# Own score buffers, a later second and third search, and output weights rounded on GpSimd, in a two-layer decoder trunk

## The chip, the cores and the metric

One core of a Trainium2 chip runs the whole forward pass. The metric is the time of one execution on the device in microseconds (us). Three runs of the kernel before are shown, and one more execution was recorded by the hardware profiler. TensorE multiplies matrices, VectorE and ScalarE do elementwise work and reductions, GpSimd does small elementwise work and issues loads on a queue of its own, SyncE (SP) issues the other transfers.

## The reference

Two layers, each a mixer and a SwiGLU, with a layer norm around each. The change touches the first mixer alone, sparse attention over 1024 positions: eight indexer heads score every causal key, each query keeps its 256 best, and 16 heads in two key groups attend to those.

```python
h = x @ w_in
c_q, k, v, k_idx, w_idx = jnp.split(h, ...)
c_q = rms_norm(c_q, g_cq)
q, q_idx = c_q @ w_uq, c_q @ w_iq
...                                        # layer norm of k_idx, rope
def attend_block(args):                    # 128 queries
    rel = relu(einsum('bqhd,bsd->bhqs', qib, k_idx))
    score = where(causal, einsum('bqh,bhqs->bqs', wb, rel), -inf)
    _, sel = lax.top_k(score, 256)
    valid = sel <= t_pos
    ...                                    # k_sel, v_sel: the chosen keys
    logits = einsum('bqgrd,bqkgd->bqgrk', qg, k_sel) * 64 ** -0.5
    p = softmax(where(valid, logits, -inf))
    return einsum('bqgrk,bqkgd->bqgrd', p, v_sel)
out = lax.map(attend_block, ...)
return out @ w_o
```

## The kernel before

The 1024 positions are eight tiles of 128 queries. The gather of the reference is replaced by a mask: for each tile an array `bias` (queries by causal keys) holds 0 for a chosen key and a huge value for another, and attention runs over all causal keys. Tiles 0 and 1 have at most 256 causal keys and need no choice. Tiles 2 to 7 need three steps.

**Index.** `index(j)` computes the scores of tile j: for each of eight indexer heads and each chunk of keys (one chunk up to tile 3, two from tile 4 on), three matmuls (high and low parts of the operands), a Relu on ScalarE (L1406), and an accumulation on VectorE into the score buffer `sc` (L1409 for the first head, L1411 for the others). Operands `it` are loaded from device memory on GpSimd's queue (L1392), two loads for two heads. A chunk is one step of the generator: 8, 8, 16, 16, 16, 16 steps for tiles 2 to 7.

**Search.** `search((3, 2))`, `((5, 4))` and `((7, 6))` find the 256th best score of each query, two tiles at a time, one on ScalarE and one on VectorE. Ten rounds of bisection count the scores above a bound (L1479, L1480). The finish (L1493 to L1501) copies the scores below the bound into a scratch tile (`za`, `zv`), takes the best eight of them (MAX8), replaces them (MATCH_REPLACE8), and writes the mask with a Relu on ScalarE. A verdict follows: a column `bad` is sent through a small transfer (L1512) to one row, GpSimd sums it (L1517), and only if it isn't zero a repair, `search_all`, runs inside a branch (L1520). Whatever reuses a buffer of the search waits for that branch, whether it is entered or not. A search is 25 steps.

**Attention.** `att_main` runs tiles 0 to 7, for each the two key groups (half tiles), for each eight heads: logits on TensorE (L1775), mask and minimum on VectorE (L1777), Exp on ScalarE (L1779), transposes (L1746), copies (L1748), the product with V (L1751). At the end of a half tile VectorE inverts the sums (L1785). From tile 6 on V is used in split form: `values()` casts its eight key tiles into score and scratch buffers that are free by then (L1689 on ScalarE, the low part L1690 on VectorE). The query operands `qt` are loaded on GpSimd's queue (L1676), four heads ahead. The output weights W_o are loaded in the second half of tile 0 (L1590, SP's queue), and `prepare` (L1596, L1597) splits them into high and low parts in the first half of tile 1: the high part a rounding on ScalarE, the low part a subtraction on VectorE, and then SP loads x into the same place (L1599). `att_out` (matmuls into `W`, L104 to L106) multiplies a finished tile with them.

**What sets the order.** Before attention comes `att_in`, the projections, by a list written out by hand (`ORDER_IN`); at each `a` in it, `STEPS` says how many steps of the index and the search generators follow. In attention, after each head, `PLAN[j]` gives the index and search steps per head of tile j, added up until a whole step is due. At the end of a tile the next tile's search is driven to its end if it isn't done. That is the order in which the program is written. The tile framework then orders each engine's instructions ahead of time: what was written earlier goes first, but work that it takes to be ready is pulled forward where it takes an engine to be idle. The score buffers are `sc0` to `sc3`, tile j in `sc{j % 4}`: tile 6 takes over tile 2's and tile 7 tile 3's, and `indexes` holds tiles 6 and 7 back until the search of tiles 2 and 3 is written and five further slots have passed (`s.now`, `s.ended`).

Of the kernel before, what the change touches and what calls it, by code (L numbers as in the profile page):

```python
# [10 lines left out]
F32 = mybir.dt.float32  # L11
F32R = mybir.dt.float32r
BF16 = mybir.dt.bfloat16
F16 = mybir.dt.float16
# [7 lines left out]
P = 128  # L22
# [39 lines left out]
class Core:  # L62
# [1104 lines left out]
        q4 s1 a k3 q5 s4 a a s5 a q6 a a q7 s6 a a s7 a a"""  # L1167
    STEPS = [(4, 0), (4, 0), (4, 0), (4, 1), (0, 2), (4, 2), (4, 2), (4, 2), (5, 2), (4, 3), (5, 3), (5, 3), (5, 3), (5, 0)]

    PLAN = [(1, 0.4), (0.6, 0.4), (0.8, 0.5), (0.4, 0.5), (0, 1), (0, 1), (0, 0), (0, 0)]  # L1170
    LATE = [10, 3, 3, 6, 8, 5, 11]

    def att_in(self, ap, csp, tp, x):
# [186 lines left out]
            s.stored = max(s.stored, t)  # L1360

        s.idx_ps = self.ps_c
        s.index, s.find, s.stored, s.now = self.indexes(), self.searches(), -1, 0
        steps = iter(self.STEPS)

        def advance():
            s.now += 2
            for gen, n in zip((s.index, s.find), next(steps)):
                for _ in range(n):
                    next(gen, None)  # L1370
# [10 lines left out]
    def index(self, j):  # L1381

        nc, v, gp, s = self.nc, self.nc.vector, self.nc.gpsimd, self.att
        bp = s.sel
        nch, n = self.chunks(j)
        S = nch * n
        sc = self.tile(bp, [P, S], F32, f"sc{j % 4}")

        def load(k):
            it = [self.tile(bp, [P, 2, P], F32R, f"it{i}", bufs=2) for i in range(2)]  # L1390
            for i in range(2):
                gp.dma_start(it[i], s.ids[j][i][:, 2 * k : 2 * k + 2, :])  # L1392
            return it

        its = [load(0)]
        for h in range(8):
            if h % 2 == 0 and h < 6:
                its.append(load(h // 2 + 1))
            w = s.wi[:, j, h : h + 1]
            for c in range(nch):  # L1400
                kr = slice(c * n, (c + 1) * n)
                ps = s.idx_ps()[:, :n]
                it = tuple(x[:, h % 2, :] for x in its[h // 2])
                self.mm3(ps, it, (s.kih[:, kr], s.kil[:, kr]), True, True)
                r = self.tile(bp, [P, n], F32, "rel", bufs=2)
                nc.scalar.activation(r, ps, AF.Relu)  # L1406
                o = sc[:, kr]
                if h == 0:
                    v.tensor_scalar(o, r, w, 0.0, op0=ALU.mult, op1=ALU.add)  # L1409
                else:  # L1410
                    v.scalar_tensor_tensor(o, r, w, o, op0=ALU.mult, op1=ALU.add)  # L1411
                if h == 7 and c == nch - 1:
                    last = sc[:, S - P :]
                    gp.affine_select(last, last, [[-1, P]], ALU.is_ge, LOWEST, base=0, channel_multiplier=1)
                    s.sc[j] = sc
                yield

    def indexes(self):
        for j in range(2, NT):
            s = self.att  # L1420
            while j > s.stored or (j >= 6 and (j - 4 not in s.done or s.now < s.ended + 5)):
                yield
            yield from self.index(j)

# [28 lines left out]
    def search(self, js):  # L1453


        nc, v, gp, s = self.nc, self.nc.vector, self.nc.gpsimd, self.att
        bp = s.sel
        scs = [s.sc.pop(j) for j in js]
        Sa, Sv = (sc.shape[1] for sc in scs)
        small = lambda tag, *shape, dt=F32, **kw: self.tile(bp, [P, *(shape or (2,))], dt, tag, **kw)  # L1460
        z = [self.tile(bp, [P, T], F32, x) for x in ("za", "zv")]
        st, mv, sd = small("sst", 2, 2, 6), small("smv", 2, 2), small("ssd")
        for i, (j, sc) in enumerate(zip(js, scs)):
            m = 1 if j * P <= 512 else 2
            n = j * P // m
            for c in range(m):
                v.bn_stats(st[:, i, c, :], sc[:, c * n : (c + 1) * n])
            v.bn_aggr(mv[:, i, :], st[:, i, :m, :].rearrange("p a b -> p (a b)"))
            yield
        v.tensor_scalar(sd.bitcast(I32), mv[:, :, 1].bitcast(I32), 0.5, 532676608.0, op0=ALU.mult, op1=ALU.add)  # L1470
        wide, half = small("wide", 1), small("half", self.ROUNDS)
        v.tensor_tensor(wide, sd[:, 0:1], sd[:, 1:2], op=ALU.max)
        v.tensor_scalar(half, s.halves[:, : self.ROUNDS], wide, None, op0=ALU.mult)
        cnt, rej, at = (small(x, bufs=2) for x in ("cnt", "rej", "at"))
        v.scalar_tensor_tensor(at, s.starts[:, js[1] : js[1] + 2], wide, mv[:, :, 0], op0=ALU.mult, op1=ALU.add)
        yield
        junk = [s.bias[j] for j in js]
        for k in range(self.ROUNDS):
            nc.scalar.activation(junk[0], scs[0], AF.Sign, bias=at[:, 0:1], scale=-1.0, accum_out=cnt[:, 0:1])  # L1479
            v.tensor_scalar(  # L1480
                junk[1], scs[1], at[:, 1:2], float(Sa - Sv - TOPK), op0=ALU.is_lt, op1=ALU.add,
                accum_out=cnt[:, 1:2],
            )
            yield
            v.tensor_scalar(rej, cnt, float(Sa - 2 * TOPK), half[:, k : k + 1], op0=ALU.is_gt, op1=ALU.mult)
            up = half[:, min(k + 1, self.ROUNDS - 1) :][:, :1]
            v.scalar_tensor_tensor(at, at, up, rej, op0=ALU.add, op1=ALU.subtract)
        acc, bad = small("acc"), small("bad")
        for i, (j, sc) in enumerate(zip(js, scs)):
            y, over = z[i][:, : sc.shape[1]], small("over", 1)  # L1490
            v.tensor_scalar(s.bias[j], sc, at[:, i : i + 1], 0.0, op0=ALU.is_gt, op1=ALU.add, accum_out=over)
            yield
            v.scalar_tensor_tensor(y, s.bias[j], -(2.0**127), sc, op0=ALU.mult, op1=ALU.add)  # L1493
            yield
            next8, void = small("next8", 8), small("void", 8)
            v.max(next8, y)
            v.tensor_scalar(void, s.needles, over, 2.0**127, op0=ALU.is_lt, op1=ALU.mult)
            v.tensor_tensor(next8, next8, void, op=ALU.add)
            yield
            v.match_replace(y, next8, y, -(2.0**127))  # L1500
            nc.scalar.activation(  # L1501
                s.bias[j], y, AF.Relu, bias=s.lift, scale=2.0**-20, accum_out=acc[:, i : i + 1]
            )
            yield
        for i, sc in enumerate(scs):
            v.scalar_tensor_tensor(
                bad[:, i : i + 1], acc[:, i : i + 1], 3 * sc.shape[1] * self.UNIT, s.kept,
                op0=ALU.subtract, op1=ALU.not_equal,
            )
        v.tensor_tensor(bad[:, 0:1], bad[:, 0:1], bad[:, 1:2], op=ALU.add)  # L1510
        row, whole = self.tile(bp, [1, P], F32, "row"), self.tile(bp, [1, 1], I32, "whole")
        nc.sync.dma_start(row, bad[:, 0:1])  # L1512
        for _ in range(3):
            yield
        n = P // 2
        while n:
            gp.tensor_tensor(row[:, :n], row[:, :n], row[:, n : 2 * n], op=ALU.add)  # L1517
            n //= 2
        gp.tensor_copy(whole, row[:, :1])
        with self.tc.If(gp.value_load(whole, min_val=0, max_val=2 * P) > 0):  # L1520
            self.search_all(js, scs, z)
        s.done.update(js)
        s.ended = s.now
        yield

    def search_all(self, js, scs, z):
# [25 lines left out]
        for bit in range(31, -1, -1):  # L1552
            part, step = full[bit < 16], float(1 << bit % 16)
            ts(cand, part, step, None, op0=ALU.add)
            bound(cand if bit >= 16 else keys, cand if bit < 16 else keys2)
            for i, sc in enumerate(scs):
                n = sc.shape[1]
                ts(z[i][:, :n], sc, least[:, i : i + 1], None, op0=ALU.is_ge)
                total(z[i], n, cnt[:, i : i + 1])
            ts(cnt, cnt, float(TOPK), step, op0=ALU.is_ge, op1=ALU.mult)  # L1560
            tt(part, part, cnt, op=ALU.add)
        bound(keys, keys2)
        for i, (j, sc) in enumerate(zip(js, scs)):
            n = sc.shape[1]
            a, b = (x[:, :n] for x in z)
            th, room = least[:, i : i + 1], cnt[:, i : i + 1]
            ts(a, sc, th, None, op0=ALU.is_gt)
            total(a, n, room)
# [14 lines left out]
    def att_main(self, bp, x, g, b):  # L1583
# [8 lines left out]
        def prepare(k):  # L1592

            h, l = oh[k // 4][:, k % 4, :], ol[k // 4][:, k % 4, :]
            r = self.resid[:, k, :]
            nc.scalar.copy(h, r)  # L1596
            v.tensor_tensor(l, r, h.bitcast(F32), op=ALU.subtract)  # L1597
            wo.append((h, l))
            nc.sync.dma_start(self.resid[:, k, :], x[k * P : (k + 1) * P, :])  # L1599
# [24 lines left out]
        for j in range(NT):  # L1624
# [6 lines left out]
            for gi in range(2):  # L1631
# [3 lines left out]
                for h in range(8):  # L1635
# [6 lines left out]
                    if (j, gi) == (1, 0):  # L1642
                        prepare(h)
                    tick()
                    s.now += 1
                    for i, gen in enumerate((s.index, s.find)):
                        owed[i] += self.PLAN[j][i]
                        while owed[i] >= 1:
# [32 lines left out]
    def values(self):  # L1681

        s = self.att
        slots = ["za"] * 4 + ["zv"] * 2 + ["sc0"] * 2
        wide = {x: self.tile(s.sel, [P, slots.count(x), 2, P], F32R, x) for x in dict.fromkeys(slots)}
        s.vhl = [wide[x][:, slots[:k].count(x)] for k, x in enumerate(slots)]
        for x, y in zip(s.vhl, range(NT)):
# [246 lines left out]
```

## Time and profile before

| | |
|---|---|
| three runs, median (lowest to highest) | 2547.21 us (2544.34 to 2547.54) |
| the profiled execution | 2549.61 us, span 2547.8 us |
| mean granted clock of TensorE | 0.988 |
| busy: TensorE, VectorE, ScalarE, GpSimd | 97%, 75%, 42%, 6% of the span |
| sparse attention, from the first tile's heads to the last | about 180 to 590 us |

The page's second part cuts the span into 40 slices of 64 us; a row of digits gives an engine's busy share in tenths, PEclk the clock granted to TensorE. In rows of the timeline the first two numbers are the start and the duration in us, and the bracket at the end says how long the engine was idle before and what released it. "POOLq L1520" is GpSimd's sequencer at the branch of the verdict. Rows with "min/median/max" give durations in ns. The name `sc` stands for all score buffers, since buffer numbers are left out.

### The profile page before, as it was taken

The page shows a single profiled execution, that of the slowest core. Times are in us where ns is not written, and L with a number is a line of the kernel's source. Part 1 is how long each engine was busy: PE and PEld are TensorE (multiplying, and loading weights), DVE is VectorE, ACT ScalarE, POOL GpSimd, SP SyncE. Part 2 cuts the span into 40 slices and gives each one's busy share as a digit, 9 for nine tenths or more (in the row PEclk, how much of TensorE's full clock was granted, in tenths as well). Part 3 has the DMA queues.
Part 4 walks back from the last instruction along what each step waited for, and adds up shares of the span by engine and source line. Part 5 has one row for each costly group of instructions (what it writes and reads, how often), then busy time and mean ns, then how long its engine had stood idle before and what let it go on. Part 6 is the DMA issues. An engine that isn't in the chain of part 4 may idle for free.

```text
span 2547.8 us, 36363 instructions
## 1 busy us (share of the span) xinstructions
PE 2475.8 (97%) x13078; PEld 2073.0 (81%) x13078; DVE 1904.8 (75%) x3745; ACT 1070.7 (42%) x2012; POOL 158.2 (6%) x317
## 2 busy tenths in 40 slices
PE   8979999999999999999999999999999999999998
PEld 8868788887888888888788888887778888888886
DVE  7788584786888667666878888887879866765767
ACT  5567576565323333333553333333353333333431
POOL 0121100000000000000011111111000000000000
PEclk9988999999999999999999999999999999999999
DMA  4475101001896233665421111113628832336853
GB/s 147 122 204 180 30 26 51 22 26 66 284 308 215 87 111 104 224 213 181 163 91 43 70 42 55 42 54 105 214 100 297 271 121 89 102 114 217 291 179 120
DMA packets 160588, 342.59 MB, mean 134 GB/s; under 512 B 18736, under 2 KB 42000, under 8 KB 152720
## 3 DMA queue, kind: packets, MB, share of 16 engines
q1 hardware_dynamic: 147728, 325.44, 38.2%
q0 software_dynamic: 12672, 14.77, 2.3%
q8 instruction: 103, 1.69, 0.3%
q14 instruction: 85, 0.70, 0.1%
HBM read 233.65 MB, written 106.43 MB: 133 GB/s over the span
## 4 chain that ended last, share of the span: by engine, by line
PE 73%; DVE 6%; DMA 2%; ACT 2%; issue 1%; SPq 0%; POOL 0%; DVEq 0%; ACTq 0%; POOLq 0%
PE Y L106 11%; PE Y L104 11%; PE Y L105 11%; PE M L104 8%; PE M L106 8%; PE M L105 8%; PE M L1042 2%; PE M L329 2%; PE L L1775 1%; PE O L1722 1%; DVE w L448 1%; PE O L1751 1%; PE Y L329 1%; PE M L1027 1%; PE T L1711 1%
## 5 line engine op out<-in xcount | busy, mean ns | idle before, releaser
L447 ACT CAST w<-raw 128x512 fp32r<-128x512 f32 (+1 forms) x373 | 289.1, 776 | 518.0 <-PE Y L106 292.2
L448 DVE TENSOR_TENSOR w<-raw,w 128x512 fp32r<-128x512 f32 (+1 forms) x373 | 327.8, 882 | 181.0 <-ACT w L447 178.0
L104 PE MATMUL Y<-x,w 128*128 128x512 f32 (+1 forms) x1120 | 432.8, 386 | 0.6 <-ACT x L447 0.6
L106 PE MATMUL Y<-x,w 128*128 128x512 f32 (+1 forms) x1120 | 426.9, 381 | 4.4 <-DVE w L448 4.4
L105 PE MATMUL Y<-x,w 128*128 128x512 f32 (+1 forms) x1120 | 429.6, 384 | 0.0
L106 PEld LDWEIGHTS Y<-x,w 128*128 128x128 f32 x1120 | 211.4, 189 | 43.7 <-DVE w L448 5.0
L104 PE MATMUL M<-x,w 128*128 128x512 f32 (+1 forms) x644 | 245.4, 381 | 1.3 <-DVE e L481 1.3
L105 PE MATMUL M<-x,w 128*128 128x512 f32 (+1 forms) x644 | 244.8, 380 | 0.0
L106 PE MATMUL M<-x,w 128*128 128x512 f32 (+1 forms) x644 | 244.5, 380 | 0.0
L104 PEld LDWEIGHTS Y<-x,w 128*128 128x128 f32 x1120 | 211.7, 189 | 37.9 <-ACT x L447 0.8
L105 PEld LDWEIGHTS Y<-x,w 128*128 128x128 f32 x1120 | 211.7, 189 | 36.5
L447 ACT CAST w<-s 128x512 fp32r<-128x512 f32 x180 | 111.8, 621 | 300.6 <-PE Y L106 119.6
L448 DVE TENSOR_TENSOR w<-s,w 128x512 fp32r<-128x512 f32 x180 | 124.4, 691 | 51.8 <-ACT w L447 51.1
L104 PEld LDWEIGHTS M<-x,w 128*128 128x128 f32 x644 | 121.0, 188 | 25.4 <-DVE e L481 2.1
L105 PEld LDWEIGHTS M<-x,w 128*128 128x128 f32 x644 | 121.0, 188 | 23.0
L106 PEld LDWEIGHTS M<-x,w 128*128 128x128 f32 x644 | 121.0, 188 | 22.9
L1775 PE MATMUL L<-ks,qt 128*128 128x512 f32 (+5 forms) x384 | 112.0, 379 | 7.1 <-DVE nm L1777 4.0
L104 PE MATMUL Y<-w 128*128 128x512 f32 x284 | 112.3, 396 | 0.2 <-ACT ph L447 0.2
L105 PE MATMUL Y<-w,w 128*128 128x512 f32 x284 | 111.7, 393 | 0.0
L106 PE MATMUL Y<-w,w 128*128 128x512 f32 x284 | 111.4, 392 | 0.0
L1779 ACT ACTIVATE p<-p,nm 128x128 f32<-128x128 f32 (+7 forms) x120 | 90.6, 756 | 40.0 <-DVE nm L1777 38.3
L1751 PEld LDWEIGHTS O<-vv,pT 128*128 128x128 f32 x672 | 90.0, 201 | 19.0 <-ACT pT L1748 16.4
(480 smaller groups left out, 5237.2 us busy)
## 6 DMA issues: line engine op xcount, KB each, us to landing
raw<-in_wgu_dram SPq DMA_DIRECT2D x44, 1024.0 KB, 6.2
wdt<-in_wd_dram SPq DMA_DIRECT2D x44, 512.0 KB, 5.4
raw<-in_wd_dram SPq DMA_DIRECT2D x66, 256.0 KB, 4.4
raw<-in_hw_dram SPq DMA_DIRECT2D x16, 1024.0 KB, 4.8
qd<-qx SPq DMA_DIRECT2D x64, 128.0 KB, 2.6
qt<-qd POOLq DMA_DIRECT2D x32, 256.0 KB, 3.0
t5q<-wdt SPq DMA_DIRECT2D x26, 256.0 KB, 5.7
t7q<-wdt SPq DMA_DIRECT2D x26, 256.0 KB, 5.8
```

Of the source, the lines that this page charges most:

```text
L104: mm(out, a[0], b[0], start=first, stop=False, **kw)
L105: mm(out, a[0], b[1], start=False, stop=False, **kw)
L106: mm(out, a[1], b[0], start=False, stop=last, **kw)
L329: mm(y[:, c], x[:, c], self.ident, **flags)
L447: self.nc.scalar.copy(hi, x)
L448: (eng or self.nc.vector).tensor_tensor(lo, x, hi.bitcast(F32), op=ALU.subtract)
L1027: nc.tensor.matmul(pl[:, n, :], kk[:, m : m + P], y[:, n, :], start=True, stop=True)
L1042: nc.tensor.matmul(pl[rows, n, cols], lhs, rhs, start=True, stop=True)
L1711: nc.tensor.transpose(pt[:, (2 * k + e) * P : (2 * k + e + 1) * P], ps[e][:, c : c + P], self.ident)
L1751: nc.tensor.matmul(po[:, h * 64 : (h + 1) * 64], pT[:, i * P : (i + 1) * P], s.vv[:, k, gi * 64 : (gi + 1) * 64], start=k == 0, stop=k == j,)
L1775: nc.tensor.matmul(ps, s.qt[:, h % 4, :], s.ks[gi][i][:, kr], start=i == 0, stop=i == 1)
L1779: nc.scalar.activation(p, p, AF.Exp, bias=nm, scale=-1.0, accum_out=sm[:, h : h + 1])
```

## The change

Each score buffer has its own place: tiles 2 and 3 use `sc4` and `sc5`, tiles 4 to 7 `sc0` to `sc3`. The index generator no longer waits for the first search. The search's finish has one scratch tile, `za`, for both of its tiles; the repair uses `za` and, as its second scratch, the mask's own storage read as 16-bit numbers. V's split form goes to `sc0` (key tiles 0, 1), `sc5` (2, 3) and `za` (4 to 7) instead of `za`, `zv` and `sc0`. `PLAN` is new: index steps per head in tiles 0 to 3 are 0.9, 0.4, 0.5, 0.3 (were 1, 0.6, 0.8, 0.4), search steps 0, 0.2, 0.7, 0.8 (were 0.4, 0.4, 0.5, 0.5). The rounding of W_o goes from ScalarE to GpSimd.

Worked out from the generators: nine chunks of tile 6 are now written before attention, the index ends early in tile 2 (was late in tile 3), the second search begins at the end of tile 1 (was in tile 0) and its verdict stands at the very end of tile 3 (was three heads earlier); the third verdict moves from the last head of tile 5's first half to the first head of its second half. The first search is written as before but for its verdict's branch, which moves from tile 0 to the second half of tile 1.

```diff
-    PLAN = [(1, 0.4), (0.6, 0.4), (0.8, 0.5), (0.4, 0.5), (0, 1), (0, 1), (0, 0), (0, 0)]
+    PLAN = [(0.9, 0), (0.4, 0.2), (0.5, 0.7), (0.3, 0.8), (0, 1), (0, 1), (0, 0), (0, 0)]
 ...
-        s.index, s.find, s.stored, s.now = self.indexes(), self.searches(), -1, 0
+        s.index, s.find, s.stored = self.indexes(), self.searches(), -1
 ...
-        sc = self.tile(bp, [P, S], F32, f"sc{j % 4}")
+        sc = self.tile(bp, [P, S], F32, f"sc{j % 4 if j >= 4 else j + 2}")
 ...
-            while j > s.stored or (j >= 6 and (j - 4 not in s.done or s.now < s.ended + 5)):
+            while j > s.stored:
                 yield
 ...
-        z = [self.tile(bp, [P, T], F32, x) for x in ("za", "zv")]
+        z = self.tile(bp, [P, T], F32, "za")
 ...
-            y, over = z[i][:, : sc.shape[1]], small("over", 1)
+            y, over = z[:, : sc.shape[1]], small("over", 1)
 ...
-                ts(z[i][:, :n], sc, least[:, i : i + 1], None, op0=ALU.is_ge)
-                total(z[i], n, cnt[:, i : i + 1])
+                ts(z[:, :n], sc, least[:, i : i + 1], None, op0=ALU.is_ge)
+                total(z, n, cnt[:, i : i + 1])
 ...
-            a, b = (x[:, :n] for x in z)
+            a, b = z[:, :n], s.bias[j].bitcast(F16)
 ...
-            nc.scalar.copy(h, r)
+            gp.tensor_copy(h, r)
             v.tensor_tensor(l, r, h.bitcast(F32), op=ALU.subtract)
 ...
-        slots = ["za"] * 4 + ["zv"] * 2 + ["sc0"] * 2
+        slots = ["sc0"] * 2 + ["sc5"] * 2 + ["za"] * 4
```

More of the change, by code (lines that the diff above doesn't have):

```diff
@@ L1362, in att_in @@
         s.idx_ps = self.ps_c
-        s.index, s.find, s.stored, s.now = self.indexes(), self.searches(), -1, 0
+        s.index, s.find, s.stored = self.indexes(), self.searches(), -1
         steps = iter(self.STEPS)
         def advance():
-            s.now += 2
             for gen, n in zip((s.index, s.find), next(steps)):
@@ L1522, in search @@
         s.done.update(js)
-        s.ended = s.now
         yield
@@ L1644, in att_main @@
                     tick()
-                    s.now += 1
                     for i, gen in enumerate((s.index, s.find)):
```

## The prediction

> **What bounds the kernel now.** I read the page's clock line, then the busy time by stage, then the order of time around each hole of TensorE in the attention part, and last the waits. (Columns of the second block: PE, PEld, DVE, ACT, POOL busy us with instructions, granted clock, DMA share, GB/s.)
>
> ```profile
> span 2547.8 us, 36363 instructions
> ...
> PEclk9988999999999999999999999999999999999999
> ```
> ```profile
> 155.00:185.00 30.00, 23.25 (x114) 18.70 (x114) 24.73 (x67) 18.99 (x43) 7.77 (x16) 0.87 0.81 212
> 185.00:215.00 30.00, 22.94 (x107) 20.95 (x108) 16.16 (x61) 17.62 (x63) 4.64 (x14) 0.56 0.66 230
> 215.00:240.00 25.00, 24.43 (x150) 20.07 (x149) 23.82 (x61) 22.57 (x58) 6.55 (x13) 1.00 0.69 219
> ```
>
> The clock line has its lasting dip in the third and fourth slice only. From 155 to 215 us TensorE is idle for 13.8 us, and from 185 to 215 its granted clock is 0.56, so some 26 of those 30 us run at half speed (0.44 of missing clock over 0.5). Outside, TensorE is full: 24.43 of 25 us already from 215 to 240. This hole is the change from projections to attention: the last of the projections, the scoring of tiles 5 and 6, the end of the first search, and tile 0's heads. What TensorE does there is work that needn't be done later; what it doesn't do is lost. The rest of the kernel can't gain from the change except at two more small holes.
>
> The first hole's centre is a wait for the first search's verdict:
>
> ```profile
> 182.38 0.52 SPq L1512 DMA_DIRECT2D row<-bad  x1
> ...
> 186.78 0.18 POOL L1519 CAST whole<-row 1x1 int32<-1x1 f32 x1
> 190.46 0.45 DVE L1409 TENSOR_SCALAR sc<-rel,wi 128x448 f32<-128x448 f32 x1 [4.29 <-POOLq L1520]
> ...
> 191.18 0.69 PE L1775 MATMUL L<-ks,qt 128*128 128x128 f32 x2 [3.60 <-DVE nm L1777]
> ```
>
> VectorE stands 4.29 us because tile 6's scores (448 columns, so tile 6) go into tile 2's buffer, which the repair branch of the search (L1520) might still read. Behind it waits tile 0's softmax, and TensorE 3.60 us. From the issue of the row's transfer to the release are 8.1 us (190.46 less 182.38).
>
> The other two verdicts stall as well, though nothing scores then:
>
> ```profile
> 270.64 0.50 SPq L1512 DMA_DIRECT2D row<-bad  x1
> ...
> 278.23 0.50 ACT L1689 CAST sc<-vv 128x128 fp32r<-128x128 f32 x2 [4.28 <-POOLq L1520]
> ...
> 279.16 0.91 PE L1751 MATMUL O<-vv,pT 128*128 128x64 f32 x6 [3.50 <-ACT pT L1748]
> ```
> ```profile
> 394.52 0.30 ACT L1689 CAST za<-vv 128x128 fp32r<-128x128 f32 x1 [3.72 <-POOLq L1520]
> ...
> 454.94 0.20 DVE L1785 RECIPROCAL sm<-sm 128x8 f32<-128x8 f32 x1
> ```
>
> Here it is ScalarE that waits, for the casts of V (`values`), which the program writes only at tile 6, that is at 454.94 us (the twelfth half tile's end). They ran at 278 and 394. So the order on an engine isn't the order of the program: work is pulled forward to where its buffer was thought to be free, and each such guess was about 4 us early. A verdict is waited for by whatever is next to reuse the search's buffers.
>
> **The change part by part.**
>
> *Scores in buffers of their own, and the index no longer held back.* In the trace the scoring of tile 6 begins at 176.57 us, as soon as its operands are there, and then goes at one chunk in 2.3 us (181.16 less 176.57, over two).
>
> ```profile
> 176.57 0.47 PE L104 MATMUL I<-kih,it 128*128 128x448 f32 x1 [0.25 <-DMA it<-id]
> ...
> 181.16 0.47 PE L104 MATMUL I<-kih,it 128*128 128x448 f32 x1
> ```
> ```profile
> 190.00:212.00 22.00, 1.78 (x3) 0.51 0.67 236
> 212.00:243.00 31.00, 7.70 (x12) 1.00 0.69 213
> ```
> ```profile
> 212.17 0.20 DVE L1785 RECIPROCAL sm<-sm 128x8 f32<-128x8 f32 x1
> ...
> 242.92 0.20 DVE L1785 RECIPROCAL sm<-sm 128x8 f32<-128x8 f32 x1
> ...
> 295.96 0.20 DVE L1785 RECIPROCAL sm<-sm 128x8 f32<-128x8 f32 x1 [0.93 <-ACT p L1779]
> ...
> 340.65 0.20 DVE L1785 RECIPROCAL sm<-sm 128x8 f32<-128x8 f32 x1
> ```
>
> The second block is VectorE's accumulation of scores (L1411) by window: 3 from 190 to 212, then 12. Tile 6 has 16 chunks, two of them first ones (L1409), so of its 14 accumulations only two or three came before tile 0's end at 212.17. Counted through the generators, the program of the change places 9 chunks before attention and 14 in tile 0: 23, against 7 before. The start can't move (176.57 waited for operands), so the pace decides. From 176.57 to 212 are 35.4 us; at 2.3 us a chunk 15 fit, less one or two for VectorE's other work, against about five now (two first ones, three accumulations): 8 more than now, to be taken as the middle. A chunk is three matmuls, and matmuls of 512 columns start 0.23 us apart:
>
> ```profile
> 269.35 0.39 PE L106 MATMUL W<-xh,otl 128*128 128x512 f32 x1
> 269.58 0.39 PE L104 MATMUL W<-xh,oth 128*128 128x512 f32 x1
> ```
>
> So 8 x 3 x 0.23 = 5.5 us of TensorE work come out of the full stretch behind 215 us and into the hole. Ends: nothing, if operands or VectorE don't follow, and 18 chunks (23 less 5), 12.4 us. Denser work should also end the half-speed stretch sooner; the 22.94 us busy there at half speed hold about 10 us to be had (0.88 of it, halved), and I take 1.5 (ends 0 and 10). [...]
>
> *The first verdict.* Tile 6 no longer waits for it. But tile 3's scores now lie in `sc5`, and the V casts of key tiles 2 and 3 reuse that buffer. By the two later verdicts, these casts will be pulled right behind the first one. I count 0: the 4 us wait goes from VectorE to ScalarE. Ends: 3.6 us gained (TensorE's hole) if ScalarE has other work there, and 0, since nothing makes the verdict later but the program's place for it, at tile 1.
>
> *Second and third search later.* Every instruction of them stays; they lose rank to the index. The second verdict is now placed behind the last head of tile 3, its row's transfer three heads earlier. Tile 3 takes 44.7 us (340.65 less 295.96), 2.8 us a head, so 8.4 us stand against the 7.6 that the second verdict took (278.23 less 270.64). If they run as ranked, tile 4's first softmax just doesn't wait. They have run ahead of their place so far. I take 0; ends 0 and +7.6. The third verdict has the second half of tile 5 as cover: 0.
>
> *One finishing buffer.* The second tile's write waits for ScalarE's Relu over the first's:
>
> ```profile
> L1501 ACT ACTIVATE bias<-za,marks x3: 723/927/1161, 171.0 to 375.9; 128x512 bf16<-128x512 f32 x1, 128x768 bf16<-128x768 f32 x1, 128x1024 bf16<-128x1024 f32 x1
> ```
>
> At most 0.93 + 0.19 us three times, 3.4; what waits behind it is heads' work that can be ordered ahead, so 0 (ends 0 and +3.4). The repair branch with its 16-bit scratch isn't entered in the trace, and the V casts are as many: 0.
>
> *GpSimd rounds W_o.* ScalarE loses eight casts, 8.4 us; GpSimd gains eight of 128x1024.
>
> ```profile
> L1596 ACT CAST xh<-resid x8: 1031/1044/1061, 207.1 to 228.5; 128x1024 fp32r<-128x1024 f32 x8
> ```
> ```profile
> L988 POOL CAST lvl<-kt x2: 506/559/612, 1301.7 to 1305.4; 128x512 uint8<-128x512 int32 x1, 128x384 uint8<-128x384 int32 x1
> ```
> ```profile
> 33.58 1.22 DVE L1212 TENSOR_TENSOR w_iql<-sc,w_iqh 128x1024 fp32r<-128x1024 f32 x1
> 34.17 0.92 POOL L190 COPY rope<-rope 128x128 f32<-128x128 f32 x1 [31.12 <-ACT rope L189]
> ...
> 35.41 0.29 POOL L190 COPY rope<-rope 128x128 f32<-128x128 f32 x1
> ```
>
> GpSimd's casts took 0.506 and 0.612 us for 384 and 512 columns, so 1.04 for 1024: 8.3 us. A 128x128 copy took 0.29 us, but 0.92 when VectorE was in a subtraction of two SBUF operands: that ended at 34.80, and the copy 0.29 later. So the two engines exclude each other for such operations, and each copy may keep VectorE, which is full from 215 to 240, for 1.04 us. TensorE's own slack there is 0.6 us (25 less 24.43): ends -0.6 and +8.3, and I take +0.5, as ScalarE's saving in the same stretch (22.57 of 25 busy) offsets most of it. SP's loads of x wait for the subtraction as before and move with it.
>
> Sum: -5.5 - 1.5 + 0.5 = -6.5 us. The profiled execution took 2549.6 (its span plus 1.8); it would take 2543.1. The median of the runs is 2547.2, 2.4 under it, so I forecast 2541. About 0.2%, 5 us, can be told from no change.
>
> **The rivals.**
>
> *The first wait goes altogether* (faster still). ScalarE is loaded with tile 0's exponentials and Relus and the casts find no early place. Then the 3.6 us and more of the half-speed stretch fall too: -6.5 - 3.6 - 2 = -12, 2535. Against it: ScalarE had 12.4 us idle from 185 to 215.
>
> *Nothing to tell* (same). The moved chunks bring their operand loads along, two on GpSimd's queue for every four chunks of tiles 6 and 7, and these come late. The output weights' loads, eight of 512 KB with 7.1 us to landing, fall into the same stretch:
>
> ```profile
> 188.59 3.74 SPq L1590 DMA_DIRECT2D resid<-in_w_o_dram  x8
> ```
> ```profile
> resid<-in_w_o_dram SPq DMA_DIRECT2D x8, 512.0 KB, 7.1
> ```
> ```profile
> 194.91 0.58 POOL L1676 DMA_DIRECT2D qt<-qd  x1 [7.95 <-PE L L1775]
> ...
> 202.03 0.45 PE L1775 MATMUL L<-ks,qt 128*128 128x128 f32 x1 [2.55 <-DMA qt<-qd]
> ```
>
> A query load issued there came too late by 2.55 us. If two more operand loads are so late, 5.1 of the 6.5 us are gone: 2546. The same case holds the exclusion at its full price, -7 + 8.3 = +1.3, 2548.5. [...] I give this price a third of the case.
>
> *The copies block GpSimd's queue* (slower). GpSimd issues the query and index loads in order. If the copies, which have an almost idle engine to be pulled forward on, are ordered ahead of those loads and wait there for W_o (eight loads, issued from 188.59 on, behind which a query load took until 202), tile 0's loads at 194.91 and later go out some 5 us late each. Two are waited for in full (10 us), and the chunks' operands, on the same queue, bring no gain: 2557. It decides as soon as a copy that waits stands ahead of a load needed before 202. Against it: on ScalarE the first cast ran at 207.1 only, behind the loads.
>
> **How the numbers follow.** Forecast 0.34; first wait gone 0.21; nothing to tell 0.30; blocked queue 0.15. So faster 0.55, same 0.30, slower 0.15. Predicted is the forecast, 2541, whose own range is 2535 to 2545 (12.4 us of chunks less the clock's share; 2 us). Over all: 2532, from the first wait's removal with a little more of the clock, to 2553, inside the blocked queue's price with one load late; below lies the largest clock gain, above the full price, together about 0.2.
>
> **What would show it.** Right: from 155 to 215 us TensorE busier and the clock above 0.56; more than ten accumulations before tile 0's end; ScalarE's cast of V waiting about 4 us for L1520 at the first verdict; second and third verdict with the stalls of before. Wrong: the scoring of tile 6 no denser before 212; TensorE waiting for `qt` or `it` more than 3 us; VectorE's subtraction behind each copy 1 us late; a softmax of tile 4 that waits for L1520.

## The result, and the profile after

The changed kernel took 2533.78 us (median of five runs, 2529.09 to 2537.45), beside 2547.21 us (2544.34 to 2550.08) for the kernel before in the same comparison: a ratio of 0.9949, with a 95% interval of 0.9933 to 0.9964, or 13.4 us less. It is faster, by more than the 2541 that was forecast, and inside the range of 2532 to 2553. The profiled execution took 2537.45 us with a span of 2535.7, 12.1 less than the span before. Of all the runs reported here a single one, of the kernel before beside the last four experiments, took 9307.55 us; the ratios leave it out. Line numbers late in the file are smaller by one to three: the verdict's branch is L1519, V's cast L1686, the rounding of W_o L1594 and its subtraction L1595.

The page's first line, and its clock line:

```profile
span 2535.7 us, 36380 instructions
...
PEclk9998999999999999999999999999999999999999
```

One of the two low slices is left. The same three stretches as in the prediction, with the same columns (TensorE, its weight loads, VectorE, ScalarE, GpSimd: busy us and instructions; granted clock, DMA share, GB/s):

```profile
155.00:185.00 30.00, 26.08 (x137) 20.04 (x136) 26.09 (x63) 21.02 (x45) 8.99 (x19) 1.00 0.88 233
185.00:215.00 30.00, 22.02 (x100) 18.11 (x99) 24.72 (x54) 15.55 (x58) 14.26 (x24) 0.80 0.76 255
215.00:240.00 25.00, 24.97 (x142) 20.43 (x140) 20.07 (x53) 15.63 (x48) 7.09 (x13) 0.90 0.65 202
```

Busy time alone hides the gain, since a matmul at half the clock is busy for longer: in the change one of the index with 448 columns took 0.57 to 0.74 us from 199 to 202 us, where the granted clock was 0.50, and 0.36 to 0.47 us from 182 to 185 us, where it was 1.00. Busy time by granted clock is a rough measure of work done. For the three stretches it was 20.2, 12.8 and 24.4 us before, and is 26.1, 17.6 and 22.5 after: 8.7 us more. The attention part from there to 420 us, TensorE alone (busy us and instructions, clock, DMA share, GB/s), is two rows of before and then two of after:

```profile
240.00:340.00 100.00, 96.18 (x588) 0.98 0.12 30
340.00:420.00 80.00, 76.81 (x547) 0.96 0.14 43
```
```profile
240.00:340.00 100.00, 99.79 (x664) 1.00 0.10 28
340.00:420.00 80.00, 76.98 (x545) 0.96 0.14 47
```

That is 94.3 and 73.7 before, 99.8 and 73.9 after. Over 155 to 420 us the measure gains 8.7 + 5.5 + 0.2 = 14.4 us, where the spans differ by 12.1. It is rough: for the eight kernels of the experiments the same sum misses the difference of the spans by 0.6 to 5.6 us. It still shows two places where the time came from, the stretch up to 240 us and the second search's verdict (near 280 before); around the third verdict nothing changed.

The work that was pulled into the hole is seen in VectorE's accumulations of scores (L1411 before, L1410 after), up to 212 us; the first row is before, the second after:

```profile
0.00:212.00 212.00, 26.82 (x45) 0.92 0.58 165
```
```profile
0.00:212.00 212.00, 34.31 (x56) 0.97 0.60 170
```

Eleven more; at three matmuls of some 0.21 us each (the starts of one chunk's are 182.66, 182.87 and 183.08 us) that is about 7 us of TensorE. They were done at the cost of tile 0, whose second half ended later than at 212.17, and were paid back until the last half tile (567.86 before):

```profile
224.46 0.20 DVE L1782 RECIPROCAL sm<-sm 128x8 f32<-128x8 f32 x1
...
558.05 0.20 DVE L1782 RECIPROCAL sm<-sm 128x8 f32<-128x8 f32 x1 [1.31 <-ACT sc L1776]
```

Tile 0 ends 12.3 us later and the last tile 9.8 us earlier. The end of one tile by itself would have been the wrong thing to judge by.

The three verdicts, in order of time:

```profile
192.86 0.50 ACT L1686 CAST sc<-vv 128x128 fp32r<-128x128 f32 x2 [3.79 <-POOLq L1519]
193.85 0.74 PE L104 MATMUL I<-kih,it 128*128 128x448 f32 x1 [3.89 <-ACT rel L1405]
...
302.14 1.13 ACT L1478 ACTIVATE bias<-sc,at 128x1024 bf16<-128x1024 f32 x1
...
303.41 0.59 ACT L1745 COPY pT<-T 128x512 f32<-128x512 f32 x1
304.67 0.50 ACT L1686 CAST sc<-vv 128x128 fp32r<-128x128 f32 x2 [0.67 <-POOLq L1519]
...
368.33 0.90 ACT L1686 CAST za<-vv 128x128 fp32r<-128x128 f32 x4 [3.13 <-POOLq L1519]
...
369.76 2.14 PE L1748 MATMUL O<-vv,pT 128*128 128x64 f32 x10 [2.98 <-ACT pT L1745]
```

At the first one the wait sits now on ScalarE, in front of V's cast. Behind that cast on ScalarE stands a Relu of the index (`rel`), for which TensorE waits 3.89 us. At the second verdict ScalarE had counts of the third search (L1478) and copies of `pT` to do while the verdict came: 0.67 us instead of 4.28, and TensorE has no hole there. At the third it is nearly as before (3.13 us for 3.72, TensorE's hole 2.98 for 2.69).

Last the new cost, GpSimd's rounding and what VectorE did beside it:

```profile
197.25 3.11 DVE L1469 TENSOR_SCALAR ssd<-smv 128x2 int32<-128x2 int32 x1
197.31 3.02 POOL L1594 CAST xh<-resid 128x1024 fp32r<-128x1024 f32 x3
...
205.95 5.37 DVE L1595 TENSOR_TENSOR xl<-resid,xh 128x1024 fp32r<-128x1024 f32 x1
206.22 4.01 POOL L1594 CAST xh<-resid 128x1024 fp32r<-128x1024 f32 x4
...
212.97 0.63 PE L1772 MATMUL L<-ks,qt 128*128 128x128 f32 x2 [2.82 <-DVE nm L1774]
```

A VectorE instruction of two elements a row took 3.11 us (0.16 the two other times it runs) while three casts ran back to back beside it, and a subtraction that takes 1.17 to 1.22 us alone took 5.37 beside four. Tile 0's softmax stood behind it, and TensorE waited 2.82 us.

### The profile page after: what moved, and what is told of

It is laid out like the page before. It is cut to its first block, busy times and chain, and to the rows that moved or that the text cites. A ratio compares the mean times of both kernels' runs of the same rounds, so it can differ in the third digit from the quotient of the medians.

```text
span 2535.7 us, 36380 instructions
## 1 busy us (share of the span) xinstructions
PE 2470.5 (97%) x13078; PEld 2066.6 (82%) x13078; DVE 1911.3 (75%) x3745; ACT 1064.7 (42%) x2004; POOL 167.1 (7%) x325
## 4 chain that ended last, share of the span: by engine, by line
PE 71%; DVE 6%; DMA 4%; ACT 2%; issue 1%; SPq 0%; POOL 0%; DVEq 0%; ACTq 0%; POOLq 0%
PE Y L106 11%; PE Y L104 11%; PE Y L105 11%; PE M L104 7%; PE M L105 7%; PE M L106 7%; PE M L1042 3%; PE M L329 2%; PE L L1772 1%; PE O L1719 1%; DMA wdt<-in_wd_dram 1%; PE O L1748 1%; DVE w L448 1%; PE Y L329 1%; PE M L1027 1%
```

## The experiments

Every kernel was timed in five rounds against the kernel before, which took 2548.08 us in the comparison of the first four and 2548.39 in that of the others. The two comparisons ran on different chips, so kernels are set beside one another by their ratios to the kernel before. The theory was that releasing the index carries the gain, that ScalarE takes over the first wait, and that the rounding on GpSimd costs close to its upper bound; the rivals were that the buffers alone or the new rates carry the gain, and that the rounding is free.

**The change without the rounding on GpSimd.**

```diff
-            gp.tensor_copy(h, r)
+            nc.scalar.copy(h, r)
```

> The change with ScalarE rounding W_o as before. Theory (exclusion): GpSimd's casts hold VectorE's operations with two SBUF operands off; in the changed kernel one subtraction took 5.37 us and a 128x2 scalar operation 3.11, TensorE stood 2.82 us behind that and ran 6.8 us at half speed after it. Without the casts that goes: 3 to 6 us faster than the changed kernel, 2528 to 2531 where it is 2534. Rival (ScalarE is the fuller engine): the eight casts of 1.04 us lengthen tile 1 where ScalarE was at 22.6 of 25 us: 3 to 8 us slower than the changed kernel, 2537 to 2542.

2529.13 us (2524.22 to 2530.72), ratio 0.9919 [0.9902, 0.9936], against 0.9949 with it. The rounding costs 0.30%, 7.6 us; the two intervals overlap by 0.0003 only, and two more comparisons below show the same sign. VectorE's subtractions are back at 1.22 us, and the stretches do more:

```profile
L1595 DVE TENSOR_TENSOR xl<-resid,xh x8: 1175/1221/1224, 204.4 to 226.4; 128x1024 fp32r<-128x1024 f32 x8
```
```profile
185.00:215.00 30.00, 24.42 (x130) 20.56 (x129) 22.58 (x71) 22.88 (x73) 9.51 (x21) 0.89 0.85 280
215.00:240.00 25.00, 24.78 (x165) 21.51 (x163) 21.97 (x54) 20.68 (x57) 4.89 (x9) 1.00 0.62 192
```

By busy time and clock 21.7 and 24.8 us, 6.4 more than with the rounding on GpSimd. ScalarE is 22.88 us busy instead of 15.55, and TensorE does better all the same.

**The kernel before, with only the rounding moved to GpSimd.**

```diff
-            nc.scalar.copy(h, r)
+            gp.tensor_copy(h, r)
```

> The kernel before with nothing changed but GpSimd rounding W_o. Exclusion: VectorE loses up to 8.3 us from 195 to 235, 2 to 8 us slower than before, 2549 to 2555. Rival (ScalarE's relief decides): 1 to 5 us faster, 2542 to 2546.

2554.31 us (2547.05 to 2563.46), ratio 1.0020 [1.0007, 1.0033]: slower, by 5 us. Beside the casts two of VectorE's accumulations took 2.99 us, where one takes 0.68 in the kernel before. But a hole of TensorE's that the kernel before doesn't have, 3.59 us near 233, has another cause. The load of the layer norm's weights is issued on GpSimd's queue at 224.44 us (218.01 before), and came behind VectorE's place for it:

```profile
208.47 2.99 DVE L1411 SCALAR_TENSOR_TENSOR sc<-rel,wi,sc 128x448 f32<-128x448 f32 x2
```
```profile
233.00 0.28 DVE L388 TENSOR_TENSOR gb<-gb 4x128 f32<-4x128 f32 x1 [5.12 <-DMA gb<-in_lnb_dram]
...
233.68 0.80 PE L1775 MATMUL L<-ks,qt 128*128 128x256 f32 x2 [3.59 <-DVE nm L1777]
```

This is the third rival's mechanism, a load that goes out late on GpSimd's queue, on another load than the one it named. That the casts made it late is not shown: right ahead of it the queue waited 4.83 us for the buffer of an index operand. So these 5 us can't all be put down to VectorE and GpSimd excluding each other. In the change the same load goes out at 226.69, and VectorE doesn't wait for it.

**The change with the old rates.**

```diff
-    PLAN = [(0.9, 0), (0.4, 0.2), (0.5, 0.7), (0.3, 0.8), ...]
+    PLAN = [(1, 0.4), (0.6, 0.4), (0.8, 0.5), (0.4, 0.5), ...]
```

> The change with the rates of the kernel before. Theory (own buffers and no hold-back carry the gain): nine chunks still stand before attention and the hole is filled nearly as well; the second search has its old place, so its verdict may be waited for again (3.5 us of TensorE and 3.4 us at half speed): 2535 to 2541. Rival (the ranks carry it): within 3 us of the kernel before, 2544 to 2550.

2541.03 us (2538.0 to 2548.06), ratio 0.9970 [0.9959, 0.9981]. The new rates are worth 0.21% here, though the intervals overlap a little. The time is at the upper end of what was expected, but not for the reason named: ScalarE doesn't wait at the second verdict here. TensorE has a hole of 3.67 us at 210.46 instead, behind an index operation on VectorE that took 3.05 us beside three casts of 3.00.

**The buffers alone.** The kernel before with `sc4` and `sc5`, one scratch and V's new slots; the index is held back, the rates and the rounding on ScalarE are the old ones. The next experiment differs from this one by the hold-back alone.

```diff
-        sc = self.tile(bp, [P, S], F32, f"sc{j % 4}")
+        sc = self.tile(bp, [P, S], F32, f"sc{j % 4 if j >= 4 else j + 2}")
 ...
-        z = [self.tile(bp, [P, T], F32, x) for x in ("za", "zv")]
+        z = self.tile(bp, [P, T], F32, "za")
 ...
-        slots = ["za"] * 4 + ["zv"] * 2 + ["sc0"] * 2
+        slots = ["sc0"] * 2 + ["sc5"] * 2 + ["za"] * 4
```

> The kernel before with the change's buffers alone (own score buffers, one finishing scratch, V in sc0, sc5 and za); hold-back, rates and rounding as before. Theory (the fill needs the index released, and the first verdict's wait only changes hands to ScalarE's cast of V): within 3 us of before, 2544 to 2550. Rival (buffers alone carry the gain, since the order on the engines is by readiness): 5 us faster or more, under 2542.

2545.38 us (2544.61 to 2550.67), ratio 0.9992 [0.9983, 1.0002]: nothing to tell for the three together; they aren't told apart. VectorE waits for no verdict any more, and ScalarE does, twice at full length (the waits; us in total, times, longest):

```profile
ACT sc L1689 <- POOLq L1520: 9.3, 2, 5.0
```
```profile
185.00:215.00 30.00, 21.61 (x111) 19.32 (x112) 15.11 (x57) 17.27 (x63) 5.33 (x14) 0.64 0.63 218
```

The wait went from one engine to the other, at the same price, as the prediction had it.

**The change with the old rates and the rounding on ScalarE.** This is the kernel of the experiment above with the hold-back taken out.

```diff
-            while j > s.stored or (j >= 6 and (j - 4 not in s.done or s.now < s.ended + 5)):
+            while j > s.stored:
```

> Own buffers and the index released, with the rates of before and ScalarE rounding. Theory (release of the index carries most, the rates the rest): GpSimd's rounding cost 7 us and the rates gave 6 with it, so without both some 2535, 12 us faster than before. Rival (the rates matter only because they clear VectorE for GpSimd's casts): 2527 to 2531, as the variant with the new rates and ScalarE rounding.

2535.12 us (2530.81 to 2538.32), ratio 0.9948 [0.9931, 0.9965]. With the rounding on GpSimd the same kernel had 0.9970, so the rounding costs 0.22% at the old rates. Releasing the index is worth 0.44%, 11 us, with intervals well apart. Between the two traces busy time by clock grows by some 10 us from 155 to 215 us (35.2 to 45.1), which is where the hole was. Against the change without the rounding (0.9919) the new rates are worth 0.29%, 7 us, with intervals that just overlap. The engines from 225 to 275 us, first with the old rates, then with the new ones:

```profile
225.00:250.00 25.00, 23.11 (x138) 18.33 (x137) 24.19 (x73) 21.19 (x55) 3.46 (x7) 1.00 0.32 99
250.00:275.00 25.00, 23.59 (x135) 20.27 (x135) 22.75 (x65) 16.36 (x39) 1.06 (x2) 0.93 0.08 22
```
```profile
225.00:250.00 25.00, 24.75 (x156) 20.80 (x155) 21.91 (x63) 18.47 (x52) 2.71 (x6) 1.00 0.30 95
250.00:275.00 25.00, 25.00 (x154) 21.30 (x153) 22.67 (x63) 18.07 (x43) 1.38 (x3) 1.00 0.08 22
```

With the old rates VectorE is 24.19 of 25 us busy from 225 to 250, just when the output weights are split and tile 0's and 1's softmaxes run, and TensorE isn't full. Its three longest waits from 225 to 275 us are for VectorE, 2.4 us together, and behind the last one its clock is 0.66 from 255 to 260; with the new rates it has no wait over 0.3 us there. Two of the three:

```profile
232.25 0.50 PE L105 MATMUL W<-xl,oth 128*128 128x512 f32 x1 [0.85 <-DVE xl L1595]
...
254.30 0.45 PE L1772 MATMUL L<-ks,qt 128*128 128x384 f32 x1 [1.17 <-DVE nm L1774]
```

The second search's counts are there as well: all but the first of its ten on VectorE (the rows of 128x640) run from 215.1 us on, with the new rates from 240.9 on:

```profile
L1479 DVE TENSOR_SCALAR_CACHE_REDUCE bias<-sc,at x19: 827/1137/1150, 215.1 to 304.7; 128x896 bf16<-128x896 f32 x10, 128x640 bf16<-128x640 f32 x9
```
```profile
L1479 DVE TENSOR_SCALAR_CACHE_REDUCE bias<-sc,at x19: 833/1137/1148, 240.9 to 317.5; 128x896 bf16<-128x896 f32 x10, 128x640 bf16<-128x640 f32 x9
```

The second verdict's wait is short in both (1.19 us with the old rates, 1.25 with the new), so that came with the release and not with the rates. The new rates change the index's steps as well as the search's, and no run has the one without the other; that the later search carries the 7 us is read from the trace.

**Where the first verdict's wait goes when V's cast is moved away.** From here on the rounding is on ScalarE and the rates are the new ones. V's key tiles 2 and 3 go to two operand buffers of the index instead of `sc5`; nothing of the first search reads those.

```diff
-        slots = ["sc0"] * 2 + ["sc5"] * 2 + ["za"] * 4
+        slots = ["sc0"] * 2 + ["it0", "it1"] + ["za"] * 4
```

> The change with ScalarE rounding, and V's key tiles 2 and 3 in two index operand buffers (it0, it1) that no search touches, instead of sc5. Theory (the first verdict is waited for by V's casts alone): ScalarE's 3.5 us wait, TensorE's hole of 3.64 and the half-speed stretch behind it go; 4 to 8 us faster than the 2529 of that variant, 2521 to 2525. Rival (something else is next to wait for the verdict, or the hole is filled late anyway): 2527 to 2531.

2530.14 us (2526.97 to 2532.58), ratio 0.9928 [0.9913, 0.9944], against 0.9919: no gain. The wait at the first verdict is gone, and the first half tile ends at 193.11 us instead of 200.56. But the second ends at 212.94 instead of 213.03:

```profile
189.68 4.25 SPq L1588 DMA_DIRECT2D resid<-in_w_o_dram  x8
```
```profile
199.79 0.77 PE L104 MATMUL I<-kih,it 128*128 128x512 f32 x1 [1.69 <-DMA it<-id]
...
202.23 0.60 ACT L1405 ACTIVATE rel<-I 128x512 f32<-128x512 f32 x1 [3.30 <-PE I L106]
```

The heads ran ahead into the time in which the eight loads of W_o fill the DMA engines (the trace gives a busy share of 1.05 from 195 to 200 us and of 1.11 to 205), and the index operands of tile 7 came late. TensorE's clock was 0.50 from 200 to 205 and 0.54 to 210, as it was 0.50 from 195 to 200 with the wait. So, as far as one trace shows, the verdict's wait hid a wait for loads.

**The same for the third verdict.** Key tiles 4 to 7 go to the operand buffers instead of `za`.

```diff
-        slots = ["sc0"] * 2 + ["sc5"] * 2 + ["za"] * 4
+        slots = ["sc0"] * 2 + ["sc5"] * 2 + ["it0", "it1"] * 2
```

> The change with ScalarE rounding, and V's key tiles 4 to 7 in four index operand buffers instead of za. Theory: nothing waits for the third verdict any more; TensorE's hole of 2.79 us and 6.8 us at half speed go, 4 to 6 us faster than 2529, 2523 to 2525. Rival (another wait takes its place): 2527 to 2531.

2526.45 us (2524.71 to 2532.14), ratio 0.9915 [0.9899, 0.9932]. V's cast waits at the first two verdicts only, and TensorE has no hole at the third, where it stood 2.79 us without this edit. From 340 to 400 us busy time by clock is 59.9 us instead of 53.7. But from 185 to 215 it is 19.9 instead of 21.7: a query load came 2.80 us late at 205 us, against 0.76 without the edit. Whether the edit made it late isn't shown. The time lies between the two that were expected; against 0.9919 the ratio is 1 us better, and the intervals can't tell the two apart.

**Let the engine wait that has time.** GpSimd splits V, so that it waits for its own verdict.

```diff
-            self.nc.scalar.copy(x[:, :, :64], vv)
-            self.nc.vector.tensor_tensor(x[:, :, 64:], vv, x[:, :, :64].bitcast(F32), op=ALU.subtract)
+            self.nc.gpsimd.tensor_copy(x[:, :, :64], vv)
+            self.nc.gpsimd.tensor_tensor(x[:, :, 64:], vv, x[:, :, :64].bitcast(F32), op=ALU.subtract)
```

> The change with ScalarE rounding, and V split on GpSimd (cast and subtraction of 128x128, eight each). GpSimd waits for its own branch, so neither ScalarE nor VectorE is held by a verdict. Theory: the first and third holes go, less about 2 us of exclusion by sixteen short operations: 2519 to 2525. Rival (exclusion costs as much as with the rounding): 2529 to 2534.

2525.86 us (2523.96 to 2530.92), ratio 0.9915 [0.9899, 0.9931]. This version has the lowest median of all and beats both kernels: it lies below the change's interval. It stands 0.9 us above the range of the theory. Against the change with only the rounding undone the ratios differ by 1 us, well within the intervals. GpSimd alone waits for verdicts; TensorE's longest wait near the first is 1.90 us instead of 3.64, and TensorE is full from 215 to 240 us and over the third verdict:

```profile
POOL sc L1686 <- POOLq L1519: 7.5, 2, 4.0
```
```profile
215.00:240.00 25.00, 25.00 (x170) 21.81 (x169) 21.97 (x59) 20.27 (x59) 4.35 (x8) 1.00 0.49 154
...
340.00:380.00 40.00, 39.96 (x284) 35.06 (x284) 20.75 (x76) 22.37 (x54) 6.00 (x19) 1.00 0.08 21
```

## Why the prediction was right, and where it was off

The sign was right and the middle 7 us too high. Two steps that were each off by some 7 us, one to either side, stand behind that, so that the time lies inside the range is in part luck:

| step | taken | ends | measured |
|---|---|---|---|
| buffers, one scratch, first verdict | 0 | -3.6 to +3.4 | -0.08%, 2 us, within the error |
| index released, with the clock | -7.0 | -22.4 to 0 | -0.44%, 11 us |
| second and third search later | 0 | 0 to +7.6 | -0.29%, 7 us |
| rounding on GpSimd | +0.5 | -0.6 to +8.3 | +0.30%, 8 us |
| sum | -6.5 | | -13 us |

The rows follow one chain of kernels, and each measured term is the difference of two neighbours' ratios; by their intervals the first is good to 2 or 3 us and the others to 5 or 6. In another order a term can come out smaller: the rounding at 0.20 and 0.22%, the new rates at 0.21%.

*The index.* The mechanism was right, its size too small. The prediction put eight chunks more ahead of tile 0's end at a pace of 2.3 us a chunk; eleven more accumulations ran up to the same time, and sixteen to tile 0's new end (61 against 45). The pace was no limit of the engines; with tile 6 released (448 columns), nine chunks started within 7.4 us, 0.9 us each:

```profile
176.83 0.47 PE L104 MATMUL C<-kih,it 128*128 128x448 f32 x1
...
184.18 0.37 PE L104 MATMUL I<-kih,it 128*128 128x448 f32 x1
```

The clock's term, 1.5 us, was too small as well: the granted clock was 0.56 from 185 to 215 and is 0.80, and 0.89 without the rounding. By busy time and clock the step from 0.56 to 0.80 over 22.02 busy us is 5.3 us. That is about half of the 10 us that the prediction saw at half speed. The 1.5 us were the author's estimate: no run shows the clock's part by itself, apart from that of the chunks.

*The first verdict.* Right in place and size: ScalarE's cast waits 3.79 us, and with the buffers alone nothing is gained. The rival by which the wait goes altogether came nearest to the time (2535), by luck: the wait stayed. And when it was really taken away, a wait for loads took its place, which the rival hadn't counted.

*The second and third search.* Here the prediction was wrong: 0 was taken, with ends of 0 and +7.6, and the new rates gave about -7, outside both. The prediction saw in the later search only a danger for tile 4's softmax. It left out that the counts leave the stretch from 215 to 240, in which it had itself read VectorE as full (23.82 of 25 us; 24.33 with the old rates and the index released, 21.97 with the new ones). It also took the second verdict's stall to persist, but that went with the release, as ScalarE had counts of the third search to do by then. The third verdict's stall stayed as predicted.

*The rounding on GpSimd.* The mechanism was found in the trace of before (a copy that took 0.92 us beside a subtraction and 0.29 otherwise), and its full price worked out as +8.3; then +0.5 was taken, on the ground that ScalarE's saving in that stretch would offset it. It didn't: ScalarE's time was not what TensorE waited for, and VectorE's was (2.82 us at 212.97). The measured 7.6 us are close to the upper end, and one of the prediction's own signs of being wrong, VectorE late behind the copies, came true. In the two rows of 3.11 and 5.37 us the wait lasts for several casts in a row, three of 3.02 us together and four of 4.01.

*Blocked queue.* In the change the copies stood behind the loads and not ahead of them, and TensorE waited for a query load no longer than 0.4 us. In the kernel before with the rounding alone one load on that queue did come late, and VectorE waited 5.12 us for it.

## What to carry to other kernels

Read a moved step by what it takes away from the engine that is full where it was, not only by where it might come late: here VectorE's relief was worth about as much (7 us) as the rounding's cost (8 us), and ScalarE's relief nothing that these runs show. When a wait for a flag can't be made shorter, try giving the next reuse of the guarded buffers to an engine that has nothing urgent behind it (here the gain, 1 us, couldn't be told from none), and look which transfer the freed work runs into. Try a bundle's parts one by one even if the bundle is faster: this one held an edit that gave back more than a third of the gain of the others.

## What the runs showed of the hardware

In the change VectorE didn't get its turn between back-to-back casts on GpSimd: it waited for all three of one run and all four of another, so each run cost about its sum (3.02 and 4.01 us) at once. Both a VectorE instruction of 128x2 elements (3.11 us, 0.16 without casts beside it) and one of 128x1024 (5.37 us, 1.22 at the median) were held to the end of the run: the first ended 0.03 us behind it, the second 1.09. It isn't always VectorE that waits: in the kernel before with the rounding alone one cast, 1.06 us at the median, took 2.02 beside a subtraction.

```profile
206.92 1.63 DVE L1597 TENSOR_TENSOR xl<-resid,xh 128x1024 fp32r<-128x1024 f32 x1
207.43 2.02 POOL L1596 CAST xh<-resid 128x1024 fp32r<-128x1024 f32 x1
```

At the six verdicts of the two kernels 3.0 to 3.6 us passed from the end of the rounding of the sum that decides the branch to the start of what waited behind it, though the repair wasn't entered: at the change's second verdict the row's sum was rounded at 301.50 us and the cast behind the branch began at 304.67. Most of it lies behind the branch instruction on GpSimd's queue, which itself took 0.05 us (durations in ns, then the start in us):

```profile
301.50 0.18 POOL L1518 CAST whole<-row 1x1 int32<-1x1 f32 x1
```
```profile
L1519 POOLq COMPARE_BRANCH  x1: 54/54/54, 302.1 to 302.1; - x1
L1519 POOLq EVENT_SEMAPHORE  x1: 17/17/17, 304.6 to 304.6; - x1
```

From the branch to the next instruction on the queue it was 2.5 to 2.9 us at all six. What the time is spent on isn't shown by the trace, and no run took the branch away.
